# A ninth quad in place of the last two plain tile pairs in the first product of an MLP

## The chip, the cores and the metric

The kernel runs on one core of a Trainium2 chip. The metric is the device time of one execution in microseconds (us). Below, "before" is the kernel as it stands and "after" the one with the change.

## The reference

One decoder layer on 512 positions with 1024 channels, all in float32: a normalization, three token mixers side by side with gates, a projection with a residual, and then the part that matters here, a gated MLP with a short causal convolution, and a last normalization:

```python
h = rms_norm(x, norm2_g)
up = causal_dwconv(h @ w_up, ffn_dw_w)        # w_up: 1024 x 5632, 3 taps per channel
f_gate, f_val = jnp.split(up, 2, axis=-1)     # 2816 channels each
x = x + (jax.nn.silu(f_gate) * f_val) @ w_down
return rms_norm(x, final_g)
```

## The kernel before

**Products in two parts.** To reach float32 accuracy, each operand is split into a rounded part ("hi") and the rest ("lo"), and each product is three matmuls, hi·hi, hi·lo and lo·hi. Weights come in chunks of 8 blocks of 128x128. A chunk is loaded by SP's queue, cast to `whi` on ACT (L260), and `wlo` is then either subtracted on DVE (L265) or, for some chunks, made by ACT writing -whi (L262) and a DMA on POOL's queue that adds the original weights to it (L263). `w_parts` keeps 4 such pairs; `ahead(c)` prepares the chunks up to three steps past the one that PE uses.

**Plain tiles.** `w_up` has 2 x 22 column tiles; pair j is tile j of the gate half (m = 0) and tile j of the value half (m = 1). A plain tile (`up_mm`, through `tile_mm`, L312 to L315) is 24 matmuls of 512 columns into one PSUM bank, named `up{m}{j}` (up13 is m = 1, j = 3). The first `RAW` = 4 pairs multiply inputs that lack the factor of the second normalization, since that factor, `box["r2"]`, tile n2r, is not there yet; DVE multiplies it in while it moves each of these 8 tiles out of PSUM into a tile `uu{m}{j}` (L365). The pairs from `RAW` to `PLAIN` = 6 multiply the normalized inputs h2 (tiles h20h, h20l, ...), and the convolution reads them straight from PSUM.

**Quads.** From pair 6 on, two pairs at a time go through `quad`, a scheme with seven products in place of eight. Each product is 24 matmuls of 256 columns. It uses three banks: a (of the kind "ps"), b ("qb") and c ("qc"). The products in order are b11 into a; then ACT copies a to b (L828); t1 into c, then ACT copies c to a tile p (L832); t2 added to b, and DVE writes b + p to c (L365); b21 to a; t3 to b; b22 to c; t4 to b. For the inputs it needs sums of h2 tiles, `xs0` to `xs3`, made by DVE and ACT in `x_sums`. For the weights it needs sums as well: of the seven chunks, r11, r12 and r22 are loaded, s1 is loaded and another quarter added to it by a DMA on POOL's queue (L232), and s2, s3 and s4 are subtractions on DVE (L226) before the cast. ACT and DVE then move the results to tiles `uu` (L1071, L365).

**Banks.** From the gates on, the eight PSUM banks are six of "ps", one "qb" and one "qc" (`share(ps=6, qb=1, qc=1)`). The two tiles of pair j = `RAW` - 1 = 3 are put into "qb" (up03) and "qc" (up13):

```python
ps = ps512(f"up{m}{j}", ("qb", "qc")[m] if j == RAW - 1 else "ps")
```

**Convolution.** For each tile, one Activation (L1021) and two taps on DVE (`conv_tap`, L1026), then SiLU (L1028, tiles ff) or the multiplication of the halves (L365); they go through a list `aside`, which `side(n)` empties between products.

**Transposes of the residual.** `x1_rows(t, h)` transposes four 128x128 blocks on PE into a bank (tiles xt, L1003), and ACT copies it out (L1005). Eight such groups are needed before the end: two stand after the plain pairs 4 and 5, six after the quads.

**Order.** The code's order is not the order on the engines: a scheduler reorders each engine's instructions at build time by its own estimate. On the chip each engine then runs its list in that order, each instruction waiting for what it needs.

Of the kernel before, what the change touches and what calls it, by code (L numbers as in the profile page):

```python
# [34 lines left out]
MID = 1  # L35
WARM, WIDE = 16, 256
EVERY = 1
RAW, PLAIN = 4, 6
DOWN = N_UNITS // UNIT - KF
UP = DOWN - 2 * KF  # L40
KEEP = 3
# [118 lines left out]
def trunk(ctx: ExitStack, tc: tile.TileContext, xT, wts, par, bias, sel, ident, fg, out):  # L160
# [22 lines left out]
    def t512(dt=F32, name="t"):  # L183
        return tp.tile([P, S], dt, tag="t", name=name)
# [4 lines left out]
    def ps512(name="ps", kind="ps"):  # L189
        return banks[kind].tile([P, 512], F32, tag=kind, name=name)  # L190
# [173 lines left out]
    def tt(out, a, b, op):  # L364
        V.tensor_tensor(out=out, in0=a, in1=b, op=op)  # L365
# [634 lines left out]
    def x1_rows(t, hf):  # L1000
        ps = ps512(f"xt{t}{hf}")
        for i in range(4):
            T.transpose(ps[:, i * P : (i + 1) * P], x1[hf * 4 + i][:, t * P : (t + 1) * P], ident_sb)  # L1003
        o = t512(name=f"x1t{t}{hf}")
        A.copy(o, ps)  # L1005
        x1t[t][hf] = o
# [26 lines left out]
    def conv_links(j, u):  # L1033

        for m in range(2):
            aside.append(lambda m=m: conv_first(j, m, u[m]))
            aside.append(lambda m=m: conv_tap(j, m, u[m], 0))

    def f_split(k):
        if 1 <= k < 9:  # L1040
            both = kp.tile([P, 1024], F32R, tag="kb", name=f"fb{k}")
            parts[k] = split(ff[k], None, into=(both[:, :512], both[:, 512:]))
        else:
            parts[k] = split(ff[k], f"fh{k}")
# [21 lines left out]
    for j in range(PLAIN, KF, 2):  # L1066
        u = [[t512(name=f"uu{m}{j + f}") for m in range(2)] for f in range(2)]

        def done(f, h, src):
            for m in range(2):  # L1070
                A.copy(u[f][m][:, h * HALF : (h + 1) * HALF], src[:, m * HALF : (m + 1) * HALF])  # L1071
            if (f, h) == (0, 1):
                conv_links(j, u[0])

        def sum22(b, p5):
            for m in range(2):
                o = slice(m * HALF, (m + 1) * HALF)
                tt(u[1][m][:, HALF:], b[:, o], p5[:, o], ALU.add)

        quad(xs, f"up{j}", done, sum22)  # L1080
        conv_links(j + 1, u[1])
        n = (j - PLAIN) // 2
        if n < 6:
            x1_rows((n + 2) // 2, n % 2)
        if j == KF - 4:
            f_split(0)
    side(99)
# [129 lines left out]
```

## Time and profile before

| | us |
|---|---|
| median of 3 runs (909.91 to 915.66) | 914.17 |
| the profiled execution | 914.54 |
| its span, first to last instruction | 912.8 |
| PE busy in it | 897.1 |
| DVE busy in it | 679.9 |
| ACT busy in it | 531.6 |

The profile names an instruction by its line, its engine, and what it writes and reads, with buffer numbers left out. Several instructions of one line that follow each other are often merged in a row (x8). Times in the trace are counted from the first instruction. A matmul's row is longer than its share of PE's time, since matmuls overlap; what counts is the distance between the starts.

### The profile page before, as it was taken

How to read it: one execution, taken by the hardware profiler on the slowest of the kernel's cores; microseconds unless marked ns; L12 is line 12 of the kernel's file. 1: busy time of each engine (PE TensorE's matmuls, PEld its weight loads, DVE VectorE, ACT ScalarE, POOL GpSimd, SP SyncE). 2: the span in 40 equal slices, each digit the busy share in tenths (PEclk: the TensorE clock that was granted, in tenths of full speed). 3: DMA queues.
4: the chain of work that ended last, by engine and by line, in shares of the span. 5: the costliest groups of instructions: out<-in, count | busy, mean ns of one | idle time of the engine just before them, and what ended most of it. 6: DMA issues, size and time to landing. Idle time of an engine off the chain costs nothing.

```text
span 912.8 us, 13413 instructions
## 1 busy us (share of the span) xinstructions
PE 897.1 (98%) x5223; PEld 793.9 (87%) x5223; DVE 679.9 (74%) x955; ACT 531.6 (58%) x820; POOL 88.4 (10%) x110
## 2 busy tenths in 40 slices
PE   8999999999999999899999999999999999999996
PEld 7888988988887889899989888889999999888885
DVE  6879959947999878866765644897899899942225
ACT  7655466566666768745444356775776777731214
POOL 3011111111121100000000001110000000000002
PEclk9999999999999999999999999999999999999998
DMA  9599876686797746676636558856666764432202
GB/s 320 174 197 201 180 176 148 139 185 153 178 218 169 159 92 151 172 185 162 185 74 204 200 136 190 184 121 159 174 175 163 184 164 133 153 129 94 93 0 93
DMA packets 42552, 145.32 MB, mean 159 GB/s; under 512 B 4852, under 2 KB 5240, under 8 KB 42488
## 3 DMA queue, kind: packets, MB, share of 16 engines
q1 hardware_dynamic: 30104, 99.36, 32.4%
q0 software_dynamic: 12384, 45.09, 29.7%
q8 instruction: 41, 0.67, 0.3%
q14 instruction: 23, 0.19, 0.1%
HBM read 142.34 MB, written 2.10 MB: 158 GB/s over the span
## 4 chain that ended last, share of the span: by engine, by line
PE 91%; ACT 3%; DMA 3%; DVE 2%; issue 1%; SPq 0%; POOL 0%; ACTq 0%; POOLq 0%; DVEq 0%
PE dn L1112 4%; PE dn L1113 4%; PE dn L1114 4%; PE mo L312 3%; PE mo L313 3%; PE mo L315 3%; PE up L313 2%; PE up L312 2%; PE up L315 2%; DMA wlo<-wts 2%; PE wo L315 1%; PE wo L313 1%; PE wo L312 1%; PE pv L594 1%; PE q L312 1%; PE pv L595 1%
## 5 line engine op out<-in xcount | busy, mean ns | idle before, releaser
L260 ACT CAST whi<-w 128x1024 fp32r<-128x1024 f32 (+1 forms) x110 | 110.5, 1004 | 174.2 <-PE dn L1113 67.3
L497 DVE SCALAR_TENSOR_TENSOR cc<-ca,par_sb,cc 128x512 f32<-128x512 f32 x180 | 123.9, 750 | 0.1
L265 DVE TENSOR_TENSOR wlo<-w,whi 128x1024 fp32r<-128x1024 f32 (+1 forms) x52 | 57.2, 1100 | 77.9 <-ACT whi L260 76.9
L263 POOL DMA_DIRECT2D wlo<-wts x72 | 62.6, 870 | 441.5 <-ACT wlo L262 372.3
L260 ACT CAST whi<-r 128x1024 fp32r<-128x1024 f32 x70 | 72.7, 1050 | 45.2 <-PE mo L313 10.2
L262 ACT ACTIVATE wlo<-whi 128x1024 fp32r<-128x1024 f32 x72 | 76.4, 1061 | 16.3 <-PE px L315 4.0
L265 DVE TENSOR_TENSOR wlo<-r,whi 128x1024 fp32r<-128x1024 f32 x56 | 68.1, 1219 | 5.4 <-ACT whi L260 5.3
L1026 DVE SCALAR_TENSOR_TENSOR uc<-uu,par_sb,uc 128x511 f32<-128x511 f32 (+1 forms) x72 | 52.1, 748 | 11.2 <-ACT uc L1021 10.7
L265 DVE TENSOR_TENSOR wlo<-s,whi 128x1024 fp32r<-128x1024 f32 x28 | 34.2, 1221 | 8.8 <-ACT whi L260 4.6
L260 ACT CAST whi<-s 128x1024 fp32r<-128x1024 f32 x28 | 29.3, 1045 | 15.3 <-DVE s L226 11.1
L232 POOL DMA_DIRECT2D s<-wts x14 | 12.1, 862 | 232.6 <-DMA s<-wts 109.5
L1112 PE MATMUL dn<-whi,fb 128*128 128x512 f32 x64 | 25.3, 396 | 0.0
L1113 PE MATMUL dn<-whi,fb 128*128 128x512 f32 x64 | 25.3, 396 | 0.0
L1114 PE MATMUL dn<-wlo,fb 128*128 128x512 f32 x64 | 25.3, 395 | 0.0
L1021 ACT ACTIVATE uc<-uu,par_sb 128x512 f32<-128x512 f32 x36 | 25.2, 728 | 0.0
L637 ACT ACTIVATE sc<-sc,nm 128x256 f32<-128x256 f32 (+1 forms) x32 | 15.6, 488 | 12.6 <-DVE nm L635 12.5
L365 DVE TENSOR_TENSOR xr<-wo,xr 128x512 f32<-128x512 f32 x8 | 5.5, 692 | 18.6 <-PE wo L315 16.2
L1141 POOL TENSOR_TENSOR x1t<-x1t,fg 128x512 f32<-128x512 f32 x4 | 5.5, 1387 | 142.6 <-ACT jk L1136 142.6
L226 DVE TENSOR_TENSOR r<-r,r 128x1024 f32<-128x1024 f32 x14 | 17.1, 1223 | 2.3 <-DMA r<-wts 1.9
L365 DVE TENSOR_TENSOR sg<-mo,sg 128x512 f32<-128x512 f32 x16 | 11.0, 687 | 9.9 <-PE mo L315 9.8
L226 DVE TENSOR_TENSOR s<-s,r 128x1024 f32<-128x1024 f32 x14 | 17.1, 1224 | 0.3
L226 DVE TENSOR_TENSOR r<-r,s 128x1024 f32<-128x1024 f32 x14 | 17.1, 1221 | 0.0
(3075 smaller groups left out, 3204.7 us busy)
## 6 DMA issues: line engine op xcount, KB each, us to landing
w<-wts SPq DMA_DIRECT2D x102, 512.0 KB, 3.6
wlo<-wts POOLq DMA_DIRECT2D x72, 512.0 KB, 5.7
r<-wts SPq DMA_DIRECT2D x56, 512.0 KB, 4.3
s<-wts SPq DMA_DIRECT2D x14, 512.0 KB, 4.4
s<-wts POOLq DMA_DIRECT2D x14, 512.0 KB, 8.5
xT<-xT SPq DMA_DIRECT2D x8, 256.0 KB, 5.5
xr<-xT SPq DMA_DIRECT2D x8, 256.0 KB, 5.6
out<-x1t SPq DMA_DIRECT2D x8, 256.0 KB, 2.1
```

What stands on the lines that cost most here:

```text
L260: A.copy(hi, w32s[c][:, s])
L262: anchor[0] = A.activation(lo, hi.bitcast(F32), AF.Copy, scale=-1.0).ins
L263: nc.gpsimd.dma_start(lo, wts[steps[c][1]], accum_op=ALU.add)
L265: anchor[0] = V.tensor_tensor(out=lo, in0=w32s[c][:, s], in1=hi.bitcast(F32), op=ALU.subtract).ins
L312: T.matmul(ps, w[k][0], x[k][0], start=k == 0, stop=False)
L313: T.matmul(ps, w[k][0], x[k][1], start=False, stop=False)
L315: T.matmul(ps, w[k][1], x[k][0], start=False, stop=k == n)
L497: return lambda: V.scalar_tensor_tensor(out=cacc[j], in0=apad[j][:, t : t + 512], scalar=pc(CW + j * CONF_K + t), in1=cacc[j], op0=ALU.mul ...
L1026: V.scalar_tensor_tensor(out=c[:, d:], in0=u[:, : 512 - d], scalar=pc(w + t), in1=c[:, d:], op0=ALU.mult, op1=ALU.add)
L1112: T.matmul(o, fh, wh, start=k == 0, stop=False)
L1113: T.matmul(o, fl, wh, start=False, stop=False)
L1114: T.matmul(o, fh, wl, start=False, stop=k == KF - 1)
```

## The change

`PLAIN` goes from 6 to 4: pairs 4 and 5 become the first of nine quads, and the pairs that are left plain are the four raw ones. The transposes of the residual, which had their first two groups after the plain pairs 4 and 5, all move to the first eight quads. The list of steps and the packing of the weights follow from `PLAIN`.

```diff
-RAW, PLAIN = 4, 6
+RAW, PLAIN = 4, 4
...
         quad(xs, f"up{j}", done, sum22)
         conv_links(j + 1, u[1])
         n = (j - PLAIN) // 2
-        if n < 6:
-            x1_rows((n + 2) // 2, n % 2)
+        if n < 8:
+            x1_rows(n // 2, n % 2)
```

The first places that move are right behind the raw pairs. On PE, the end of tile up13 and what follows it stood in before as:

```order
L315 MATMUL up13_5673<-xh6h_5248,wlo_119_5565 128x512
L315 MATMUL up13_5673<-xh7h_5288,wlo_119_5565 128x512
L312 MATMUL up04_5719<-h20h_5345,whi_120_5596 128x512
L313 MATMUL up04_5719<-h20l_5346,whi_120_5596 128x512
L312 MATMUL up04_5719<-h21h_5351,whi_120_5596 128x512
```

In after, the first product of the new quad (up4a, 24 matmuls) follows up13, and behind that product stand a group of transposes, one matmul of t2 into up4b, and then t1 into up4c:

```order
L1003 MATMUL xt00_5955<-ident_sb_127,xr1_4966 128x128
L1003 MATMUL xt00_5955<-ident_sb_127,xr2_4968 128x128
L1003 MATMUL xt00_5955<-ident_sb_127,xr3_4970 128x128
L814 MATMUL up4b_5753<-xs0h_5355,whi_122_5673 128x256
L814 MATMUL up4c_5755<-xs0h_5355,whi_121_5643 128x256
L815 MATMUL up4c_5755<-xs0l_5356,whi_121_5643 128x256
L814 MATMUL up4c_5755<-xs1h_5379,whi_121_5643 128x256
```

Where before had 96 matmuls of 512 columns into four banks of "ps", after goes to "qb" and "qc" right behind the first 24 matmuls.

On DVE, the moves of the raw tiles out of PSUM (uu) stood in before with taps of the convolution between them, up to the last one, uu13:

```order
L365 TENSOR_TENSOR uu12_5629<-up12_5595,n2r_5338 128x512
L365 TENSOR_TENSOR ff1_5553<-ff1_5553,uc11_5558 128x512
L1026 SCALAR_TENSOR_TENSOR ff2_5631<-uu02_5627,par_sb_102,ff2_5631 128x511
L365 TENSOR_TENSOR uu03_5705<-up03_5641,n2r_5338 128x512
L1026 SCALAR_TENSOR_TENSOR ff2_5631<-uu02_5627,par_sb_102,ff2_5631 128x510
L1026 SCALAR_TENSOR_TENSOR uc12_5636<-uu12_5629,par_sb_102,uc12_5636 128x511
L365 TENSOR_TENSOR uu13_5707<-up13_5673,n2r_5338 128x512
L1026 SCALAR_TENSOR_TENSOR uc12_5636<-uu12_5629,par_sb_102,uc12_5636 128x510
```

In after, the same place has the lo part of chunk s2 (wlo_122) and the second tap of uc12 ahead of uu13:

```order
L365 TENSOR_TENSOR uu12_5630<-up12_5595,n2r_5338 128x512
L1026 SCALAR_TENSOR_TENSOR ff2_5632<-uu02_5628,par_sb_102,ff2_5632 128x511
L265 TENSOR_TENSOR wlo_122_5674<-s_121_5601,whi_122_5673 128x1024
L1026 SCALAR_TENSOR_TENSOR ff2_5632<-uu02_5628,par_sb_102,ff2_5632 128x510
L1026 SCALAR_TENSOR_TENSOR uc12_5637<-uu12_5630,par_sb_102,uc12_5637 128x511
L365 TENSOR_TENSOR uu03_5703<-up03_5642,n2r_5338 128x512
L1026 SCALAR_TENSOR_TENSOR uc12_5637<-uu12_5630,par_sb_102,uc12_5637 128x510
L365 TENSOR_TENSOR uu13_5705<-up13_5672,n2r_5338 128x512
L365 TENSOR_TENSOR ff2_5632<-ff2_5632,uc12_5637 128x512
```

Further ahead in after, and not in this piece, stand two more instructions of the new quad's weights that before did not have there: the lo part of s1 (wlo_121) between h2y7 and h27l, and the subtraction that makes s2 (L226) right behind uu11. Between h27l and uu13, DVE's list has 26 instructions in before and 29 in after.

## Rows read from the trace of the kernel before

**Rows 1.** The page: busy time of each engine, share of the span, instructions.

```profile
PE 897.1 (98%) x5223; PEld 793.9 (87%) x5223; DVE 679.9 (74%) x955; ACT 531.6 (58%) x820; POOL 88.4 (10%) x110
```

**Rows 2.** The chain that ended last, quads of the MLP: start, us, what.

```profile
765.21 0.96 PE up20a L820 x8
...
782.32 0.94 PE up20b L820 x8
```

**Rows 3.** Timeline of PE behind the raw pairs: start, us, instruction.

```profile
597.24 0.39 PE L312 MATMUL up<-h20h,whi 128*128 128x512 f32 x1
...
608.12 0.60 PE L1003 MATMUL xt<-ident_sb,xr 128*128 128x128 f32 x4
...
619.82 0.36 PE L814 MATMUL up6a<-h20h,whi 128*128 128x256 f32 x1
...
621.81 0.28 PE L820 MATMUL up6a<-h20h,wlo 128*128 128x256 f32 x1
```

**Rows 4.** Busy time by window: length, PE, PEld, DVE, ACT, POOL, clock, DMA.

```profile
600.70:622.40 21.70, 21.70 (x111) 18.42 (x110) 21.62 (x31) 14.14 (x21) 1.73 (x2) 1.00 0.29 52
...
642.40:662.80 20.40, 20.40 (x174) 20.40 (x173) 17.96 (x22) 14.62 (x24) 1.72 (x2) 1.00 0.71 182
```

**Rows 5.** Timeline of DVE, 588 to 616 us.

```profile
588.84 0.75 DVE L996 SCALAR_TENSOR_TENSOR h2y<-xr,par_sb,n2r 128x512 f32<-128x512 f32 x1
590.27 0.69 DVE L357 TENSOR_TENSOR h27l<-h2y,h27h 128x512 fp32r<-128x512 f32 x1 [0.69 <-ACT h27h L356]
...
594.13 0.69 DVE L777 TENSOR_TENSOR xs3l<-xt,xs3h 128x512 fp32r<-128x512 f32 x1
...
606.49 0.69 DVE L365 TENSOR_TENSOR uu<-up,n2r 128x512 f32<-128x512 f32 x1
607.09 0.75 DVE L1026 SCALAR_TENSOR_TENSOR uc<-uu,par_sb,uc 128x510 f32<-128x510 f32 x1
...
613.57 1.23 DVE L265 TENSOR_TENSOR wlo<-s,whi 128x1024 fp32r<-128x1024 f32 x1
614.70 0.76 DVE L1026 SCALAR_TENSOR_TENSOR uc<-up,par_sb,uc 128x510 f32<-128x510 f32 x1
615.36 1.23 DVE L226 TENSOR_TENSOR s<-s,r 128x1024 f32<-128x1024 f32 x1
```

**Rows 6.** Timeline of PE around a wait in the stage of the gates.

```profile
386.49 0.39 PE L820 MATMUL gt00a<-hn0h,wlo 128*128 128x256 f32 x1 [1.97 <-DMA wlo<-wts]
...
388.27 0.41 PE L814 MATMUL gt00c<-xs2h,whi 128*128 128x256 f32 x1
388.49 0.41 PE L815 MATMUL gt00c<-xs2l,whi 128*128 128x256 f32 x1
```

**Rows 7.** Windows behind that wait, columns as in rows 4 (clock before the last two).

```profile
387.00:388.00 1.00, 1.00 (x9) 1.00 (x9) 1.00 (x2) 0.20 (x1) 0.00 (x0) 0.84 0.13 45
388.00:389.00 1.00, 1.00 (x7) 1.00 (x6) 1.00 (x2) 0.37 (x1) 0.00 (x0) 0.50 0.00 0
...
391.00:392.00 1.00, 1.00 (x10) 1.00 (x9) 0.00 (x0) 0.93 (x1) 0.00 (x0) 0.95 0.93 254
```

**Rows 8.** Timeline of ACT, making a quad's r11 in two parts.

```profile
671.33 1.05 ACT L260 CAST whi<-r 128x1024 fp32r<-128x1024 f32 x1 [1.13 <-PE up10a L815]
...
672.82 0.73 ACT L1021 ACTIVATE uc<-uu,par_sb 128x512 f32<-128x512 f32 x1
673.44 1.06 ACT L262 ACTIVATE wlo<-whi 128x1024 fp32r<-128x1024 f32 x1
```

**Rows 9.** Timeline of POOL behind it.

```profile
674.79 0.86 POOL L263 DMA_DIRECT2D wlo<-wts  x1 [2.02 <-ACT wlo L262]
```

**Rows 10.** Landing of the loads of line 221, 560 to 700 us.

```profile
DMA to landing us min/median/max: 3.3/4.3/8.6
```

**Rows 11.** Landing of the adding DMAs of line 263, 600 to 790 us.

```profile
DMA to landing us min/median/max: 5.6/8.0/8.4
```

## The prediction

> **What bounds the kernel now.** I read the page first: PE is busy for 897.1 of 912.8 us [rows 1], so a stage is worth what PE spends in it, plus what PE waits. Then the chain that ended last: through the quads of the MLP it runs from product to product on PE. Then the timelines around the place of the change. The two plain pairs lie between 597.24, the first matmul of up04, and 619.82, the first of quad up6 [rows 3]. PE doesn't wait in this stretch: it is busy for 21.70 of 21.70 us. But DVE is busy for 21.62 of the same 21.70, against 17.96 of 20.40 in a later quad [rows 4]. So the plain pairs are a stretch in which DVE works off what the second normalization and the raw tiles have heaped up, while PE has something to do that asks nothing of DVE. That is what the reader is to see, since the change takes this stretch away.
>
> **Step 1, PE's own work.** Two plain tiles take 608.12 - 597.24 = 10.88 us, four 21.76; the rest of 22.58 is two groups of transposes, 0.41 each [rows 3]. In quad up20 the ends of the first and the seventh product lie 782.32 - 765.21 = 17.11 apart, so a product takes 2.85 and seven take 19.96 [rows 2]. Gain: 1.80 us. The groups of transposes are eight before and after, at the same price.
>
> The Trainium skill, "TensorE: Matmul & The Clock Gate", section "Back-to-back issue gap", gives N/2.4 + 2.5 ns at full clock for a lone stream: 109 ns for 256 columns. Here it is 2.85/24 = 119 ns, so the measurement decides; by the page both kinds would be shorter and the gain 96 x 216 - 168 x 109 ns = 2.4 us, and the time 0.6 us less than below.
>
> **Step 2, the banks.** In after, PE ends up13 at 597.24 as before, runs the first product into up4a (2.85) and a group of transposes (0.41), and stands at 600.50 before one matmul into up4b and then up4c. Bank b still holds up03 and bank c up13, until DVE has run uu03 and uu13. Before, that was no matter: uu13 started at 606.49 [rows 5] and quad up6 at 619.82. The inputs are no obstacle, since the last xs tile is begun at 594.13 [rows 5].
>
> **Step 3, when uu13 ends.** DVE runs its list without pause here, so I add starts. Distances from start to start [rows 5]: a 1024-wide lo part or subtraction 1.13 (613.57 to 614.70), a tap 0.66 (614.70 to 615.36), a 512-wide TENSOR_TENSOR 0.60 (606.49 to 607.09). Up to h2y7 at 588.84 the list is the same. wlo_121 then starts at 589.50 and h27l at 590.63 in place of 590.27; it had waited 0.69 there, which covers part of it: +0.36. From h27l to uu13 there are three more: s2's subtraction (1.13), wlo_122 (1.13), a tap of uc12 (0.66); 0.18 of DVE's idle in between may be absorbed, and I take off as much. Sum 3.1: uu13 starts at 609.6 and, lasting 0.69, ends at 610.3. ACT's copy of a to b waits for uu03, which stands 1.26 us ahead of uu13 (one move, one tap); I let it end with uu13. PE waits 610.3 - 600.5 = 9.8 us. Nothing else can run on it meanwhile: its list is in order, and everything behind is this quad.
>
> **Step 4, the clock.** What a wait does to the clock is in the stage of the gates: after 1.97 us without work [rows 6] the granted clock read 0.84, 0.50 three times and 0.95 in five windows of a microsecond [rows 7], that is 0.32 + 3 + 0.10 = 3.4 us at the lower level (1.2 GHz). Matmuls of 256 columns then came 0.21 apart (388.27 to 388.49) [rows 6] in place of 0.119. A wait of 9.8 us should leave PE at the lower level when it starts again. 3.4 us hold 16 matmuls and cost 16 x 0.094 = 1.5 us. Bounds: nothing, if the clock is back at once, and 3.0 us, if it takes twice as long. I take 1.5, the one case in the trace. So of the 48 matmuls of t1 and t2, 16 take 3.4 and 32 take 3.8: done at 617.5.
>
> On this the same page of the Trainium skill, section "HAM oscillation — how this bites in real kernels", speaks against the change: a wait between bursts throttles PE, and the price is half of the throttled time. By that rule 3.4 us cost 1.7 in place of 1.5, and the time would be 0.2 us more.
>
> **Step 5, the rest of the quad.** b21 ends at 620.35. t3 needs up4b read by DVE's up4c addition: behind uu13 (609.6) stand uu13 itself, ff2, four taps, wlo_123, ff3 and three 1024-wide ones, 0.60 + 0.60 + 2.64 + 1.13 + 0.60 + 3.39 = 8.96, so the addition starts at 618.6 and is over before 620.35. t3, b22 and t4 end at 628.9, and 16 matmuls of up6a (1.9) bring PE to 630.8, where it needs wlo_127.
>
> **Step 6, the next quad's r11.** Its load takes the buffer of r21, which the subtraction for s3 frees: DVE starts that at 609.6 + 0.60 + 0.60 + 2.64 + 1.13 + 0.60 = 615.2 and it lasts 1.23, so 616.4. The load lands 4.3 later (3.3 to 8.6) [rows 10]: 620.7. From the cast of such a chunk on ACT (671.33) to POOL's issue (674.79) it takes 3.5 [rows 8, 9], of which 0.62 is an Activation of the convolution that doesn't stand there in after: 2.9, so 623.6. The adding DMA lands 8.0 later (5.6 to 8.4) [rows 11]: 631.6. PE waits another 0.8 us. Before, this matmul started at 621.81 [rows 3], with one more group of transposes (0.41) done. So from here on PE is 631.6 - 621.8 + 0.4 = 10.2 us late; as a sum, -1.8 + 9.8 + 1.5 + 0.8, within rounding.
>
> **Step 7, behind it.** The other quads and the last product have the same instructions as before, each later by this much. DVE's 18.0 of 20.4 us per quad [rows 4] is enough, and PE was busy nearly to the end, so nothing gives the delay back. Loads: seven per quad against four chunks with four adding DMAs, 7 transfers against 8; I cost them at nothing.
>
> **Sum.** 914.5 + 10.2 = 924.7 from the profiled execution, which is 0.4 above the median: 924.4 us. What three runs can tell from no change is about 1%, here 9.1 us.
>
> **Rivals.**
> - *No wait: the saved product shows* (the other side). If uu03 and uu13 were done by 600.5, the result would be 914.2 - 1.8 = 912.4 us. For it: 19.96 against 21.76 us on PE, certain; the chip runs the same number of moves. Against: uu13 started at 606.49 even without the new weights in DVE's list, and the list is fixed when the kernel is built. It decides from uu13 ending 8 us earlier than before's own order has it; DVE would have to skip a dozen instructions.
> - *The wait, but cheap.* The clock is back at once (t1 and t2 done at 616.0, b21 at 618.9, t3 held by the addition to 619.3, PE at wlo_127's place at 629.7) and the adding DMA lands early (623.6 + 5.6 = 629.2): 629.7 - 621.8 + 0.4 = 8.3 late, 922.5 us. For it: the shortest landing of this stage is that 5.6 [rows 11]. Against: the clock did fall after 1.97 us, and the median landing is 8.0.
> - *The wait, and dear.* The lower clock for twice as long, or a load that takes 8.6 and an adding DMA that takes 8.4: 616.4 + 8.6 + 2.9 + 8.4 = 636.3, 14.9 late, 929.0 us. For it: the queue of loads restarts right there with several at once. Against: each only if it falls badly.
> - *The delay lives on at each seam between quads*, because every r11 lands just in time. That would add to the dear case; against it, the later quads had no such wait, and their order is the same.
>
> **How the numbers follow.** Forecast (9.1 to 12 us late) 0.52, cheap (7 to 9.1) 0.25, dear 0.15, no wait 0.08. Slower by over 1%, from 923.3 up: nearly all of the forecast and the dear case, less some of the measurement's own spread (runs from 909.9 to 915.7): 0.62. Within 1%: the cheap case, most of no wait, and that spread: 0.36. Faster by over 1% has no mechanism, only spread: 0.02. The range leaves out no wait and half of the dear end: 919.5 to 929 us.
>
> **What would show it.** In after's trace: PE without work from about 600.5 for some 10 us, ended by DVE's uu or by ACT's copy L828; uu13 starting near 609.6; windows at a granted clock of 0.50 behind that; a second, short wait of up6a for `wlo<-wts`; every product from there at 2.85 us. The forecast is wrong if PE's wait there is under 7 us, if DVE idles before uu13, or if quads further on wait too.

## The result and the profile after

The change made the kernel slower: 925.99 us median of 6 runs (922.8 to 929.01) against 913.58 of 6 (909.91 to 917.85); the ratio is 1.0137, with a 95% interval of 1.0119 to 1.0156. The forecast was 924.4. The profiled execution of after took 924.34 us, its span is 922.5. It is the second fastest of the six (granted clock 0.991 on average, against 0.988 to 0.990 in the three slowest), so its trace shows somewhat less than the median holds.

The waits of PE over the whole span of after (line, releaser, us in total, times, longest):

```profile
PE up4b L814 <- DVE uu L365: 9.4, 1, 9.4
PE up6a L820 <- DMA wlo<-wts: 1.7, 1, 1.7
PE gt00a L820 <- DMA wlo<-wts: 1.5, 1, 1.5
...
PE up14a L820 <- DMA wlo<-wts: 0.2, 1, 0.2
```

The first two are new; the third was there before (1.97, [rows 6]). PE's busy time fell by 1.4 us, from 897.1 [rows 1] to this:

```profile
PE 895.7 (97%) x5295; PEld 796.2 (86%) x5295; DVE 692.0 (75%) x967; ACT 534.7 (58%) x828; POOL 86.8 (9%) x108
```

Busy time holds the matmuls at the lower clock too (some 2 us in after, as shown below, and 1.5 in before by [rows 7]), so this fits the 1.8 us that the quad should save; the waiting cost more. Here is the place on PE's timeline (the answer to [rows 3]); the tile after the raw ones starts at 595.58, where before had 597.24, so this execution came to the place 1.66 us earlier, and that is added wherever times of the two are compared:

```profile
595.58 0.28 PE L814 MATMUL up4a<-h20h,whi 128*128 128x256 f32 x1
...
598.46 0.60 PE L1003 MATMUL xt<-ident_sb,xr 128*128 128x128 f32 x4
...
608.46 0.58 PE L814 MATMUL up4b<-xs0h,whi 128*128 128x256 f32 x1 [9.40 <-DVE uu L365]
...
616.22 0.29 PE L814 MATMUL up4a<-h21h,whi 128*128 128x256 f32 x1
...
619.10 0.28 PE L814 MATMUL up4b<-xs0h,whi 128*128 128x256 f32 x1
...
631.42 0.39 PE L820 MATMUL up6a<-h20h,wlo 128*128 128x256 f32 x1 [1.69 <-DMA wlo<-wts]
```

One product and a group of transposes, then nothing for 9.4 us, 48 matmuls of t1 and t2 that take 7.76 us (608.46 to 616.22) where the full clock needs 5.7, and at the start of the next quad the second wait. DVE meanwhile has no gap (the answer to [rows 5]):

```profile
587.20 0.74 DVE L996 SCALAR_TENSOR_TENSOR h2y<-xr,par_sb,n2r 128x512 f32<-128x512 f32 x1
587.86 1.22 DVE L265 TENSOR_TENSOR wlo<-s,whi 128x1024 fp32r<-128x1024 f32 x1
588.99 0.69 DVE L357 TENSOR_TENSOR h27l<-h2y,h27h 128x512 fp32r<-128x512 f32 x1
...
606.47 0.70 DVE L365 TENSOR_TENSOR uu<-up,n2r 128x512 f32<-128x512 f32 x1
607.07 0.75 DVE L1026 SCALAR_TENSOR_TENSOR uc<-uu,par_sb,uc 128x510 f32<-128x510 f32 x1
607.72 0.70 DVE L365 TENSOR_TENSOR uu<-up,n2r 128x512 f32<-128x512 f32 x1
...
613.30 1.24 DVE L226 TENSOR_TENSOR r<-r,r 128x1024 f32<-128x1024 f32 x1
...
616.80 0.69 DVE L365 TENSOR_TENSOR up4c<-up4b,up4p 128x512 f32<-128x512 f32 x1
```

The two uu at 606.47 and 607.72 are uu03 and uu13: they let go the banks b and c. The copy of a to b on ACT lies between them and PE's restart:

```profile
607.20 0.72 ACT L1021 ACTIVATE ff<-uu,par_sb 128x512 f32<-128x512 f32 x1 [0.57 <-DVE uu L365]
607.83 0.58 ACT L828 COPY up4b<-up4a 128x512 f32<-128x512 f32 x1
```

The copy ends at 608.41, as uu13 does (608.42), and PE starts at 608.46. Windows of a microsecond, one in the wait and the others behind it (columns as in [rows 4]; the clock is the third number from the end):

```profile
602.00:603.00 1.00, 0.00 (x0) 0.00 (x0) 1.00 (x3) 0.72 (x1) 0.00 (x0) 0.85 0.00 0
...
608.00:609.00 1.00, 0.55 (x2) 0.55 (x3) 1.00 (x3) 0.95 (x2) 0.00 (x0) 0.50 0.00 0
...
611.00:612.00 1.00, 1.00 (x6) 1.00 (x6) 1.00 (x3) 0.63 (x1) 0.00 (x0) 0.50 0.00 0
612.00:613.00 1.00, 1.00 (x7) 1.00 (x6) 1.00 (x2) 0.00 (x0) 0.00 (x0) 0.53 0.00 0
613.00:614.00 1.00, 1.00 (x11) 1.00 (x10) 1.00 (x2) 0.29 (x1) 0.00 (x0) 1.00 0.00 0
```

The level fell during the wait and was back at about 613. The number of matmuls per window tells the same: 6 or 7 at the lower level, 11 at full clock. POOL's queue, which brings the next quad's r11 its lo part (the answer to [rows 9]), and how long such DMAs took from 560 to 790 us (to [rows 11], which begin at 600; from there on after's median is 7.9):

```profile
621.53 0.86 POOL L232 DMA_DIRECT2D s<-wts  x1 [38.95 <-PE up4b L815]
622.07 1.22 POOL L263 DMA_DIRECT2D wlo<-wts  x1
...
DMA to landing us min/median/max: 5.5/7.5/9.3
```

From there to the end of the last quad the kernel keeps its pace; the ends of the first and seventh products of quad up20 lie as far apart as in [rows 2]:

```profile
775.02 0.96 PE up20a L820 x8
...
792.12 0.94 PE up20b L820 x8
```

From the end of the raw tiles to the end of up20's seventh product after took 792.12 - 595.58 = 196.54 us and before 782.32 - 597.24 = 185.08 [rows 2, 3]: 11.5 us of the 12.4 between the medians.

### The profile page after: what moved, and what is told of

Same layout as the page of the kernel before. It is cut to its first block, busy times and chain, and to the rows that moved or that the text cites. A ratio compares the mean times of both kernels' runs of the same rounds, so it can differ in the third digit from the quotient of the medians.

```text
span 922.5 us, 13577 instructions
## 1 busy us (share of the span) xinstructions
PE 895.7 (97%) x5295; PEld 796.2 (86%) x5295; DVE 692.0 (75%) x967; ACT 534.7 (58%) x828; POOL 86.8 (9%) x108
## 4 chain that ended last, share of the span: by engine, by line
PE 86%; DVE 6%; DMA 4%; ACT 2%; issue 1%; SPq 0%; POOL 0%; POOLq 0%; DVEq 0%; ACTq 0%
PE dn L1112 4%; PE dn L1113 4%; PE dn L1114 4%; DMA wlo<-wts 3%; PE mo L312 3%; PE mo L313 3%; PE mo L315 3%; PE wo L315 1%; PE wo L312 1%; PE wo L313 1%; PE pv L594 1%; PE q L312 1%; PE pv L595 1%; PE pv L596 1%; PE px L312 1%
## 5 line engine op out<-in xcount | busy, mean ns | idle before, releaser
L260 ACT CAST whi<-w 128x1024 fp32r<-128x1024 f32 (+1 forms) x106 | 106.3, 1002 | 173.7 <-PE dn L1113 67.3
L260 ACT CAST whi<-r 128x1024 fp32r<-128x1024 f32 x75 | 77.6, 1051 | 40.4 <-PE mo L313 10.2
L263 POOL DMA_DIRECT2D wlo<-wts x69 | 60.4, 876 | 422.4 <-ACT wlo L262 353.3
L262 ACT ACTIVATE wlo<-whi 128x1024 fp32r<-128x1024 f32 x69 | 73.2, 1061 | 16.3 <-PE px L315 4.0
L265 DVE TENSOR_TENSOR wlo<-r,whi 128x1024 fp32r<-128x1024 f32 x60 | 73.1, 1220 | 4.6 <-ACT whi L260 3.3
L1026 DVE SCALAR_TENSOR_TENSOR uc<-uu,par_sb,uc 128x511 f32<-128x511 f32 (+1 forms) x76 | 55.2, 748 | 13.2 <-ACT uc L1021 12.7
L265 DVE TENSOR_TENSOR wlo<-s,whi 128x1024 fp32r<-128x1024 f32 x30 | 36.6, 1220 | 8.8 <-ACT whi L260 4.6
L260 ACT CAST whi<-s 128x1024 fp32r<-128x1024 f32 x30 | 31.4, 1046 | 14.0 <-DVE s L226 9.4
L226 DVE TENSOR_TENSOR r<-r,r 128x1024 f32<-128x1024 f32 x15 | 18.4, 1225 | 1.7 <-DMA r<-wts 1.3
L226 DVE TENSOR_TENSOR s<-s,r 128x1024 f32<-128x1024 f32 x15 | 18.4, 1224 | 0.4
L226 DVE TENSOR_TENSOR r<-r,s 128x1024 f32<-128x1024 f32 x15 | 18.3, 1222 | 0.0
```

The lines of the kernel that those rows point to most:

```text
L226: sub = lambda o, a, b: V.tensor_tensor(out=o, in0=a, in1=b, op=ALU.subtract)
L260: A.copy(hi, w32s[c][:, s])
L262: anchor[0] = A.activation(lo, hi.bitcast(F32), AF.Copy, scale=-1.0).ins
L263: nc.gpsimd.dma_start(lo, wts[steps[c][1]], accum_op=ALU.add)
L265: anchor[0] = V.tensor_tensor(out=lo, in0=w32s[c][:, s], in1=hi.bitcast(F32), op=ALU.subtract).ins
L1026: V.scalar_tensor_tensor(out=c[:, d:], in0=u[:, : 512 - d], scalar=pc(w + t), in1=c[:, d:], op0=ALU.mult, op1=ALU.add)
```

## The experiments

Theory D says that DVE is late as a whole at the place where the plain pairs stood: its list puts the convolution's taps of the raw tiles ahead of the moves out of PSUM and of the new quad's weights, and everything else follows. In all profiles below the stretch from the end of the raw tiles to the last eight matmuls of up20's sixth product ("the stretch") is taken to compare; it is 182.23 us in before (597.24 to 779.47) and 193.70 in after (595.58 to 789.28).

**The banks alone.** In after, pair 0, which DVE moves out first, takes "qb" and "qc":

```diff
-        ps = ps512(f"up{m}{j}", ("qb", "qc")[m] if j == RAW - 1 else "ps")
+        ps = ps512(f"up{m}{j}", ("qb", "qc")[m] if j == 0 else "ps")
```

> The raw pair 0 (moved out first) takes the banks qb and qc in place of pair 3, so that the quad's banks b and c are free by 593 us; DVE's list stays as in after. Theory D (DVE is late as a whole: the taps of the raw tiles stand ahead of the quad's weights): the wait moves from the banks to wlo_122 and wlo_123, which DVE ends at 605.2 and 612.8 us in after's trace; the next r11 can still be loaded only behind the subtraction for s3 (614.5), so up6a's lo part starts at about 631 us as in after: 925 us, within 2 us of after. Rival B (the two banks alone are the cause): the 9.4 us of waiting and the low clock behind them are gone, 912 to 915 us.

The ratio to before was 1.018 (1.0158 to 1.0201), from three executions of 927.31 to 931.38 us (the fourth, which was profiled, took 2289.61). The middle one, 928.63, is 2.6 us slower than after, a little outside the 2 us that I gave. One more execution of the same kernel is the one whose profile is used:

> The same kernel as e1_banks, for an undisturbed profile (in that one's profiled execution every matmul ran at a third of its rate or less). Theory D: PE's wait of 9.4 us for the banks is gone from the list of waits, and waits for wlo_122 and wlo_123 (DVE) stand in its place, with more than 6 us in sum; up6a's lo part starts no earlier against the end of the raw tiles than in after. Rival B: no waits of more than 2 us in this quad.

It took 926.82 us in one run. Its waits of PE:

```profile
PE up4a L820 <- DVE wlo L265: 5.8, 1, 5.8
PE up6a L820 <- DMA wlo<-wts: 2.4, 1, 2.4
...
PE up4b L814 <- DVE up4c L365: 1.5, 1, 1.5
```

The wait for the banks is gone, and PE waits for the lo part of r12 (wlo_123) and for the addition into up4c instead, 7.3 us in sum; the waits stand later, and the stretch is 193.65 us (597.76 to 791.41), as in after. Rival B falls: the banks are where the delay shows, not what makes it. One sign of theory D did not come as given: up6a's lo part started 34.86 us behind the raw tiles (597.76 to 632.62), 1.0 us earlier than in after (595.58 to 631.42). The clock evened that out: behind up6a's wait of 2.4 us it read 0.50 from 633 to 635, where after kept 1.00.

**The taps out of the way.** The steps of the raw pairs' convolution are left to the quads, which run 10 each in place of 9:

```diff
-        beside = slot_ if sum22 is None else lambda _: side(3)
+        turns = iter((4, 3, 3))
+        beside = slot_ if sum22 is None else lambda _: side(next(turns))
...
         conv_links(j, pss)
-        side(4)
```

> The convolution of the raw pairs is no longer run between the raw tiles (side(4) taken out); each quad runs 10 of its steps in place of 9. Banks and everything else as in after. Theory D: on DVE's list uu13 comes 16 taps and products (some 10 us) earlier, at about 598 us in after's count, before PE has ended the first product; no wait for b and c, no low clock, and no wait of up6a: before less 1.8, 911.8 us, or up to 914 if a later quad waits for DVE. Rival W (the quad's own weights are too much for DVE at this place, 7 x 1.2 us and more): the wait shrinks only by half, 918 to 921 us.

Measured: 915.21 us (912.65 to 917.42), ratio 1.0026 (1.0013 to 1.004). Its waits of PE in the quads:

```profile
PE up4b L815 <- DVE up4c L365: 0.8, 1, 0.8
...
PE up18a L821 <- DMA wlo<-wts: 0.7, 1, 0.7
...
PE up6a L821 <- DMA wlo<-wts: 0.3, 1, 0.3
```

With the same quads, banks and weights, but the taps elsewhere, the wait of 9.4 us is gone; rival W falls. But the median is 1 us above the range I gave. The profiled execution, 913.42 us, lies inside it; its stretch is 183.06 us (595.33 to 778.39), with small waits of later quads in it, so what the other executions had more is not shown. DVE's fuller list is what changed: for the wait of 0.8 us e9_first below tries it, for the later ones it is argued.

**PE kept busy in the wait.** Matmuls of zeros into a spare bank:

```diff
         product(a, "b11", True)
+        if name == "up4":
+            hold = ps512("hold")
+            for _ in range(72):
+                T.matmul(hold[:, :WIDE], zero[:, :P], zero, start=True, stop=True)
```

> 72 matmuls of zeros into a spare bank stand between the first product of the new quad and its second (8.6 us at full clock, inside the wait of 9.4), so that PE doesn't stand idle; they add nothing to the result. All theories: the granted clock stays at 1.00 from 600 to 613 us. Theory D with the chain through r11: t1 to t4 end some 1.8 us earlier, but wlo_127 lands when it did (about 631 us), since the load of s_135 and the adding DMA before it on POOL's queue don't depend on PE; the wait of up6a grows from 1.7 to 3 us or more: 925.5 us, within 0.5 us of after. Rival S (the terms add up): 1.9 us less than after, 924 us.

Measured: 926.3 us (925.96 to 929.96), ratio 1.0148 (1.0131 to 1.0165). The profiled execution is the slowest of the four; the others took 926.45 us or less. Windows of four microseconds (columns as in [rows 4]), then the group of zeros on PE and what up6a waited for, then the adding DMA:

```profile
602.00:606.00 4.00, 4.00 (x36) 4.00 (x35) 4.00 (x7) 1.74 (x3) 0.00 (x0) 1.00 0.00 0
...
610.00:614.00 4.00, 4.00 (x36) 4.00 (x36) 4.00 (x6) 1.22 (x2) 0.00 (x0) 1.00 0.00 0
...
634.00:638.00 4.00, 4.00 (x20) 4.00 (x20) 2.24 (x2) 1.21 (x2) 0.00 (x0) 0.50 0.02 4
```

```profile
597.95 8.79 PE L827 MATMUL hold<-zero 128*128 128x256 f32 x72
...
633.59 0.58 PE L820 MATMUL up6a<-h20h,wlo 128*128 128x256 f32 x1 [6.38 <-DMA wlo<-wts]
```

```profile
622.73 1.22 POOL L263 DMA_DIRECT2D wlo<-wts  x1
```

The clock stays at 1.00 up to up6a and t1 to t4 run at full speed: counted from the end of the raw tiles, PE comes to up6a's wait 2.0 us earlier than in after (627.21 - 595.08 = 32.13 against 629.73 - 595.58 = 34.15). But the time doesn't fall, since up6a now waits 6.4 us. The adding DMA, on POOL's timeline in the last fence, was issued no earlier than in after (27.65 us behind the raw tiles against 26.49), and PE went on 10.86 us behind it (633.59 - 622.73). Rival S falls for this edit alone: what the clock costs in t1 and t2 is hidden behind r11. The edit did not rid this execution of the low clock, though: it fell in the new wait and stayed at 0.50 for some 6 us of matmuls behind it (the last of these windows). So this run does not tell what the clock costs.

**No adding DMA for that r11.** In `by_dma`, the second quad's r11 is taken out, so that DVE subtracts wlo_127:

```diff
-        return kind == "r11"
+        return kind == "r11" and i != UP + 12
```

> The lo part of the second quad's r11 (wlo_127) is subtracted on DVE in place of ACT's -whi and the adding DMA. Theory D: it is there at about 621 us, up6a doesn't wait: 1.7 us less than after, 924.3 us. Rival: the wait only passes on to the next chunk (s1 or s2 of that quad), since DVE is behind by as much: same as after, 926 us.

Measured: 925.05 us (921.9 to 925.51), ratio 1.0128 (1.011 to 1.0146). The wait of up6a is gone from the list, while the first one stays at 9.4; the stretch is 192.85 us (597.55 to 790.40), 0.85 less than in after. That is half of the 1.7: one later quad (up18a) waits 1.0 us for its `wlo<-wts`, which it didn't in after. The medians differ by less than the intervals can tell.

**Both.** The two edits above together:

> e5_warm and e6_r11 together: matmuls of zeros in the wait, and wlo_127 subtracted on DVE. If the price of the low clock is real and was only hidden behind wlo_127 in e5_warm: 1.9 us less than e6_r11, 923.1 us. If the clock costs nothing here: the same as e6_r11, 925 us.

Measured: 920.6 us (919.66 to 922.4), ratio 1.0093 (1.0068 to 1.0117), lower than either figure I gave. It is 4.4 us less than e6_r11 in the medians; in the stretches of the two profiles it is 190.62 against 192.85, 2.2 us less. So the low clock had a price of about 2 us, which shows once r11 isn't in the way. What makes up the rest of the 4.4 is not shown: the profiled execution of e7_warm_r11 waited only 0.2 us at gt00a, where e6_r11's waited 2.2 and had the lower clock behind that, but how the other executions fared there is not recorded.

**The transposes alone.** Before (`PLAIN` = 6) with all groups beside the eight quads:

```diff
-        if j >= RAW:
-            x1_rows(0, j - RAW)
...
-        if n < 6:
-            x1_rows((n + 2) // 2, n % 2)
+        if n < 8:
+            x1_rows(n // 2, n % 2)
```

> Before (PLAIN = 6) with only the transposes moved: all eight groups beside the eight quads, none behind the plain pairs. Theory D and the prediction: the groups cost 0.4 us each wherever they stand: 912.5 us, no change. Rival: an added group beside the last two quads delays DVE or ACT there, 914 us or more.

Measured: 913.43 us against 913.11, ratio 1.0002 (0.9988 to 1.0016). That half of the change costs nothing.

**A version that keeps the gain.** The edit of e4_spread, with fewer steps in the first quad:

```diff
+        turns = iter((1, 3, 3) if name == "up4" else (4, 3, 3))
```

> e4_spread, but the new quad runs only 7 of the convolution's steps (1, 3 and 3) and the others 10 each, so that DVE's addition into up4c and the loads of the next quad aren't held up by taps. Theory D: the wait of 0.8 us for up4c's addition goes and those for wlo<-wts shrink: 912 to 913.5 us, before's time or up to 1.8 us less (all that PE's work can give). Rival: ten steps in each later quad hold DVE up there as in e4_spread: 915 us.

Measured: 912.22 us (910.92 to 915.68) against 913.11, ratio 0.9999 (0.9986 to 1.0011). DVE's list from 593 us on now reads:

```profile
593.17 2.48 DVE L365 TENSOR_TENSOR uu<-up,n2r 128x512 f32<-128x512 f32 x4
595.57 1.21 DVE L226 TENSOR_TENSOR s<-s,r 128x1024 f32<-128x1024 f32 x1
596.70 1.28 DVE L365 TENSOR_TENSOR uu<-up,n2r 128x512 f32<-128x512 f32 x2
597.95 1.23 DVE L265 TENSOR_TENSOR wlo<-s,whi 128x1024 fp32r<-128x1024 f32 x1
```

The moves stand first, uu13 ends at about 598, when PE ends its first product; no wait is left in this quad, and in the quads only 0.4 us. The stretch is 180.51 us (595.42 to 775.93), 1.7 less than in before, almost all of the 1.8 that PE's work can give. In the whole time that is 0.2%, and this comparison does not show it.

**The same mechanism in the gates.** The wait at gt00a [rows 6] is one for an adding DMA, too. The edit of e6_r11, for that quad's r11 (chunk 62 in the packing), in e9_first and in before:

```diff
-        return kind == "r11"
+        return kind == "r11" and i != 62
```

> e9_first, and in the stage of the gates the lo part of quad gt00's r11 subtracted on DVE in place of the adding DMA, as e6_r11 did for up6. The same mechanism as behind the new quad: the wait for wlo<-wts (1.5 to 2.7 us in most profiles) and the low clock behind it (1.5 us) go: 909 to 910 us, 3 us less than before. Rival: DVE is busy throughout that stretch, and its 1.1 us there turn up as a wait of another product: 912 us.

> Before, with that edit of gt00's r11 alone. Same mechanism: 910 to 911 us, 2 to 3 us less than before. Against e10_gate it shows what the ninth quad is worth once nothing waits: theory D says 1.8 us (e10_gate below e11_gate_before by that much), the rival nothing.

Measured beside the same runs of before (913.38): e10_gate 908.92 us (908.46 to 909.58), ratio 0.9957 (0.9941 to 0.9972); e11_gate_before 910.7 (909.83 to 912.08), ratio 0.9975 (0.9965 to 0.9984). In the place of [rows 7], a window of e10_gate shows full clock and no gap, with DVE busy all the time:

```profile
384.00:388.00 4.00, 4.00 (x36) 4.00 (x35) 4.00 (x5) 1.53 (x2) 0.00 (x0) 1.00 0.39 132
```

This edit is worth 2.7 us in before (913.38 to 910.7), within the forecast; e10_gate came 0.1 us below its own. With the wait goes what the clock did behind it: of the 17 executions of before beside these, 7 had a mean granted clock of 0.995 or 0.996 and took 913.38 to 914.46 us (the profiled one of [rows 7] had 0.995), and of the 18 with the edit one did. Between the two new kernels lie 1.8 us, what theory D gave for a ninth quad without waits, and all six executions of e10_gate lie below all twelve of e11_gate_before. Their profiles are not quite without waits: 1.2 us in e10_gate's quads (up6a and up18a), where e9_first with the same quads had 0.4, and 0.8 in e11_gate_before's. e10_gate is faster than before and after.

## Why the prediction was right

Step by step, with 1.66 us added to after's times:

- **Step 1**, the gain on PE (1.80): e9_first's stretch is 1.7 shorter and e10_gate is 1.8 below e11_gate_before. Moving the transposes costs nothing (e2_transposes). The figure of the Trainium skill, "TensorE: Matmul & The Clock Gate", section "Back-to-back issue gap", by which the gain was 2.4, is not borne out.
- **Steps 2 and 3**, the banks and DVE's list: uu13 starts at 607.72 + 1.66 = 609.38 (forecast 609.6), PE at 610.12 (610.3). From the end of the transposes, 598.46 + 0.41 = 598.87, to 608.46 it is 9.6 us (forecast 9.8); the row counts 9.40. What the text did not say is that the banks were only the first of several waits: with the banks free (e1b_banks) DVE's lo part of r12 and its addition into up4c hold PE for 7.3 us.
- **Step 4**, the clock, was sized too small: the lower level lasted from the restart to about 613, 4.5 us and not 3.4, and 48 matmuls took 2.05 us longer, not 1.5. The row that the 3.4 came from differs in one point that the forecast passed over: in the gates PE went on at 386.49 and the clock was back at about 391.1, 4.6 us later, but it fell only at about 387.7, so that the first 1.2 us ran at full clock [rows 6, 7]. Behind the long wait it had fallen before PE went on, and all 4.5 us were at the lower level. The Trainium skill's rule in "TensorE: Matmul & The Clock Gate", "HAM oscillation — how this bites in real kernels" (half of the throttled time) gives 2.25 from the 4.5 us; the trace agrees within 0.2.
- **Step 5**, the rest of the quad: t3 at 620.76 (forecast 620.35), the addition into up4c at 618.46 (618.6).
- **Step 6** is the term whose size was off most: the wait for wlo_127 is 1.69 us (forecast 0.8). The load of r11 was not what decided. POOL first issued the addition of s for that quad (621.53), and the adding DMA behind it landed 9.3 us after its issue at 622.07, the longest of its kind in this stretch of after, where I had taken the median of 8.0.
- **Step 7** held: no later quad of after's profile waits more than 0.2 us, and nothing gives the delay back. (In e6_r11 up18a waited 1.0 us, so the quads are not always free of it.)

The measured delay in the stretch is 11.5 against 10.2: -0.2 from the wait, +0.55 from the clock, +0.9 from wlo_127. Read as the chain that lands last, nearly all of it is the adding DMA: it was issued at 622.07 + 1.66 = 623.73, as forecast (623.6), and took 1.3 us longer than the median; what the clock took beyond the forecast only shortened PE's wait for it. The forecast's own range (9.1 to 12 late) holds the 11.5. The median of the runs, 12.4 later than before, lies just above that part and inside the whole range (919.5 to 929 us); where the other 0.9 us come from is not shown. The rival with no wait would have needed uu13's end at 600.5, which is 6.7 us ahead of before's own (607.18; the 8 us of the forecast's text were off) and 9.6 ahead of after's, and e9_first shows that it takes another order of DVE's list to have that.

The terms are not free of each other, which the sum passed over: the clock's 2 us and wlo_127's wait lie side by side. Keeping the clock up in t1 and t2 alone left the time as it was (e5_warm, where it fell later instead), taking wlo_127's wait away alone brought 0.9 us in the medians (e6_r11), and both together 5.4 (e7_warm_r11). In the stretches of the profiles the last is 3.1.

## What to carry to other kernels

Work on a slower path may be what gives another engine time to catch up: before replacing it, look at how busy the others are in just that stretch, and for which tiles of theirs the replacement will ask. Where freeing one resource only moves a wait, the order of the list behind it is the cause: in an in-order engine's list, put the moves that free buffers and the operands of what comes next ahead of work whose result nobody needs soon. And price a wait with what starts late behind it, the clock and the loads, by the chain that lands last and not by the sum of all.

## What was not expected of the hardware

- The adding DMAs on POOL's queue vary more than the rows before showed (5.6 to 8.4 [rows 11]): 9.3 us in after and 10.8 in e5_warm, both where the quad's loads restarted together after the wait, but also 9.3 in e6_r11 and 9.6 in e4_spread in late quads with no such restart. That they share the bandwidth was not tried by itself.
- The length of a wait alone does not tell whether the lower clock follows. At gt00a it came behind 1.97 us in before, 2.10 in e1b_banks and 2.25 in e6_r11, and not behind 2.16 in e9_first and 2.72 in e2_transposes; behind 1.69 us at up6a in after the granted clock read 1.00 from 631 to 636. What decides was not tried. Here are the wait and a window behind it, first for e2_transposes, then for e6_r11:

```profile
387.81 0.39 PE L820 MATMUL gt00a<-hn0h,wlo 128*128 128x256 f32 x1 [2.72 <-DMA wlo<-wts]
388.00:389.00 1.00, 1.00 (x10) 1.00 (x10) 1.00 (x2) 0.00 (x0) 0.00 (x0) 1.00 0.31 111
...
386.86 0.58 PE L820 MATMUL gt00a<-hn0h,wlo 128*128 128x256 f32 x1 [2.25 <-DMA wlo<-wts]
388.00:389.00 1.00, 1.00 (x7) 1.00 (x6) 0.55 (x1) 0.00 (x0) 0.00 (x0) 0.50 0.06 16
```

- From PE's restart to the return of the full clock it took 4.5 us in after, 4.6 in before's gates, 3.3 and 5.0 in e6_r11 (gates and up4b), 4.0 in e1b_banks (gates) and 5.9 in e5_warm (up6a). One case, as the forecast had, does not give the size; what sets it was not tried.
